# A decoder layer on one core: the first half's squares added by GpSimd, a third quad of weight sums made in DRAM, the gate's second-half residual added by DMA, and its root spread later

## The chip, the core and the metric

The kernel runs on one core of a Trainium2 chip. The metric is the time of one execution in device microseconds (us), the median of several runs. The engines are TensorE (PE in the profile; its weight loads are PEld), VectorE (DVE), ScalarE (ACT), GpSimd (POOL) and SyncE (SP). Each takes its instructions in order from a queue of its own. SP, ACT and POOL also issue DMAs; a DMA that adds to its destination (`accum_op`) is issued from POOL.

## The reference

One layer over 1024 positions of width 1024: a mixing block with its output projection, a squared-ReLU MLP and a gated embedding, each added to the residual.

```python
h = h + jnp.concatenate([y_a, y_b, y_c], axis=-1) @ w_out[i]
f = jnp.square(jax.nn.relu(rms_norm(h, norm2_g[i]) @ w_ff1[i]))
h = h + f @ w_ff2[i]
gate = jax.nn.sigmoid(rms_norm(h, norm3_g[i]) @ w_ple_gate[i])
h = h + gate * (p[i] @ w_ple_proj[i])
```

All is float32. `y_a`, `y_b` and `y_c` come from a gated convolution, eight heads of stick-breaking attention and a spatial-gating MLP.

## The kernel before, in words

Activations are held transposed, features on the 128 partitions and 512 positions (a half) in a tile. A float32 product is three matmuls of rounded parts: every operand is split into `hi` (a cast on ACT, line 138) and `lo` (a subtraction on DVE, line 139). The three large products after the mixing block are done as 2x2 blocks with seven block products instead of eight; their operands are sums of weight blocks ("S1" to "S4") beside plain blocks ("A11", "A12", "A22").

The order of instructions on each engine is set by a scheduler that runs a model of the program; `tc.issue_after(x)` holds an instruction behind x in that order. Tiles come from pools: `raw` (4 buffers), `sum` (6), `tmp` (12) and `w` (22) in the late part, where eight pairs of `w` hold the parts of `y` for a while.

The stages that the change touches:

- **Output projection** (lines 881 to 928). Two halves of eight blocks, in the order n = 0, 4, 1, 5, 2, 6, 3, 7. Each block is 24 matmuls into `o_ps`. SP loads its two weight tiles and the residual `xt`; DVE adds `o_ps` to `xt` (line 908); ACT stores it to `h_dram`, scales it to `hg` and squares it (line 845); POOL adds the square to `S2[h]` by an accumulating DMA (line 849). The last two squares of the second half are kept apart.
- **Roots.** `root_of` sums `S2` over the partitions on PE (`ms_ps`, line 858), DVE forms `ms` (861), POOL the power -1/2 `r` (174), DVE `diag` (866). `spread_root` spreads it by a matmul (`R_ps`, 873) and an ACT copy (874). The first half's root stands in PE's order behind the second half's third block.
- **Sums of weights** (`up_sums`, line 786). After the square of each block but the first of each half and the last two, one step of `STEPS` makes part of the sums of a quad in `u_sums`, in DRAM: copies on ACT's queue, accumulates on POOL's. Four steps make a quad; there are twelve chances for a step. Quads 0 and 1 are made so; for all later quads SP loads a block and POOL adds others to it in SBUF (`add_up`, line 798). `events` gives each load, add and split a place among the products of the up projection, seven slots to a quad, and `supply` issues them.
- **Up projection** (line 943 on). For each of 16 quads PE makes seven products; ACT copies the first bank to `v` (line 961) before PE adds to that bank again.
- **Gate** (line 1179 on). Seven products over four blocks j in the order of `GATE`. `gated` (1161) multiplies by the root, takes the sigmoid, multiplies by `pp` and adds the residual on DVE, then stores; the stores go from POOL except for two tiles. The second half's root is taken at product 1, j = 1, and spread at product 1, j = 3.

Of the kernel before, what the change touches and what calls it, by code (L numbers as in the profile page):

```python
# [10 lines left out]
ALU = mybir.AluOpType  # L11
# [5 lines left out]
KT = D // P  # L17
# [15 lines left out]
def hybrid_block(ctx: ExitStack, tc: tile.TileContext, a: dict):  # L33
# [5 lines left out]
    nc = tc.nc  # L39
# [130 lines left out]
    def cols(parts, sl):  # L170
        return parts[0][:, sl], parts[1][:, sl]
# [41 lines left out]
    S1 = halves("S1")  # L213
# [543 lines left out]
    def add(eng, out, x, y):  # L757
        return eng.tensor_tensor(out=out, in0=x, in1=y, op=ALU.add)  # L758
# [7 lines left out]
    def run(bank, w, b, first, last, part=slice(None)):  # L766


        w, b = w[part], b[part]
        for k, ((lh, ll), (rh, rl)) in enumerate(zip(w, b, strict=True)):  # L770
            for i, (l, r) in enumerate(((lh, rh), (lh, rl), (ll, rh))):
                done = nc.tensor.matmul(bank, l, r, start=first and k == 0 and i == 0,  # L772
                                        stop=k == len(b) - 1 and i == 2, skip_group_check=True)
        return done
# [5 lines left out]
    FIRST = (1, 2, 6, 5, 7, 3, 4)  # L780
    raw_of, up_pairs = {}, {}

    EARLY = 2
    u_sums = dram.tile([EARLY, 4, P, HT], F32, name="u_sums")

    def up_sums(i, behind_add, behind_act):
# [20 lines left out]
    for q in range(FT):  # L807
        base = 7 * (q - 1)
        sums = ((-6, load_up, "S1", "A21"), (-4, add_up, "S1", "A22"),
                (-4.1, load_up, "S2", "A11"), (-2, add_up, "S2", "S1"),  # L810
                (-1.1, load_up, "S3", "A11"), (1, add_up, "S3", "A21"),
                (0.1, load_up, "S4", "A12"), (2.1, add_up, "S4", "S2"))
        if q < EARLY:
            sums = tuple((at, load_up, to, to) for at, to in zip(
                ((2, 2.1, 3.4, 3.45), (-0.9, -0.89, 0.9, 2))[q], ("S2", "S1", "S3", "S4")))
        events += [(base + at, what, q, *args) for at, what, *args in sums + (
            (-2.1, load_up, "A11", "A11"),
            (3.8 if q == 0 else 2, load_up, "A12", "A12"), (4, load_up, "A22", "A22"))]
        for k, p in enumerate(UP if q else FIRST):
            events.append((base + k + 0.5 if q else (-3.5, -0.99, -0.98, -0.97, -0.96, -0.4, -0.3)[k],  # L820
                       pair_up, q, p))
# [18 lines left out]
    def late_squares(acc, src, first, by_dma=False, apart=False):  # L840
        if first:
            nc.scalar.activation(acc, src, AF.Square)
            return
        sq = late_slot("tmp", "sq")
        nc.scalar.activation(sq, src, AF.Square)
        if apart:
            return sq
        if by_dma:
            return nc.gpsimd.dma_start(acc, sq, accum_op=ALU.add)
        return add(nc.gpsimd, acc, acc, sq)  # L850
# [30 lines left out]
    for h in range(2):  # L881
        for n in (0, 4, 1, 5, 2, 6, 3, 7):
            end = h == 1 and n in (3, 7)
            if h == 1:

                if n == 5:
                    with tc.issue_after(block_end.ins):
                        diag = root_of([S2[0]], "20")
                elif n == 6:
                    with tc.issue_after(block_end.ins):  # L890
                        spread_root(diag, R2[0])
                supply({4: -12, 1: -10, 5: -8, 2: -6, 6: -4, 7: -3}.get(n, -100))
            wu = first_wu[n] if h == 0 and n in first_wu else plain_units(a["w_out"][n])
            if end:
                xt = fetch(a["xT"][n * P:(n + 1) * P, half[h]], "sum")
            else:
                xt = slot("xt")
                nc.sync.dma_start(xt, a["xT"][n * P:(n + 1) * P, half[h]])
            o_ps = late_bank("o_ps")
            block_end = product(o_ps, [(wu[k], y_parts[h][k]) for k in range(KT)])  # L900
            if h == 0:
                i = len(y_parts[1])
                src = fetch(y_dram[i, 1], "sum") if i < 6 else y_a[i - 6][1]
                y_parts[1].append(two_parts(src, lambda s: late_slot("w", f"y_{s}", F32R)))
            if h == 1 and n == 7:
                supply(-0.975)

            evicted = add(nc.vector, xt, o_ps, xt)
            nc.scalar.dma_start(h_dram[n, h], xt)
            t = hg[n][h] = late_slot("tmp", "hg")  # L910
            scaled = nc.scalar.activation(t, xt, AF.Copy, scale=g2[:, n:n + 1])
            summed = late_squares(S2[h], xt, n == 0, True, end)
            if end:
                last_sqs.append(summed)
            elif summed:
                up_sums(up_step[0], summed, scaled)
                up_step[0] += 1
            if h == 1 and n == 7:
                supply(-0.955)
            j = n % 4  # L920
            if h == 0:
                hn[1 if n < 4 else 2][j] = hn_pair(t)
            elif n >= 4:
                b11, b12, b21 = hg[j][0], hg[j][1], hg[n][0]
                t2 = late_slot("tmp", "t2")
                token_sums(b11, b12, b21, t, nc.vector, b11, t2, b12, b21)
                for p, src in ((6, t2), (5, b11), (7, b12), (3, t), (4, b21)):
                    hn[p][j] = hn_pair(src)
# [229 lines left out]
                parts = w_pair(src)  # L1158
                yield [unit(parts, k) for k in range(4)]

    def gated(n, h, src, t, c, sign=1.0):

        nc.vector.tensor_tensor(out=t, in0=src, in1=R3[h][:, c], op=ALU.mult)  # L1163
        nc.scalar.activation(t, t, AF.Sigmoid, scale=sign)
        nc.vector.tensor_tensor(out=t, in0=t, in1=pps[n, h][:, c], op=ALU.mult)  # L1165
        add(nc.vector, t, t, h_res[n][h][:, c])
        queue = nc.sync if (n, h) in ((KT - 1, 0), (KT - 2, 0)) else nc.gpsimd
        queue.dma_start(a["out"][n * P:(n + 1) * P, half[h]][:, c], t)

    def bring_pp(n, h):  # L1170
# [8 lines left out]
    for p in GATE:  # L1179
        for j in range(4):  # L1180

            cs = pieces if p in (7, 4) and j == 3 else whole
            banks = (d_bank.pop((MATE[p], j)) if p in MATE
                     else [late_bank("g_ps")[:, :c.stop - c.start] for c in cs])
            if p in (1, 3, 7):
                d_bank[p, j] = banks
            w_of.append(next(w_made, None))
            w = w_of.pop(0)
            if p == 2:
                bring_pp(j, 0)  # L1190
            elif p == 5:
                bring_pp(j, 1)
            elif p in (7, 4):
                bring_pp(j + 4, 1 if p == 7 else 0)
            for bank, c in zip(banks, cs):
                run(bank, w, [cols(b, c) for b in h3[p]], p not in MATE, p not in (1, 7))
                if p == 1:
                    v_of[j] = late_slot("tmp", "v")
                    nc.scalar.copy(v_of[j], bank)
                elif p == 2:  # L1200
                    gated(j, 0, bank, late_slot("tmp", "gt"), c)
                elif p == 6:
                    subtract(nc.vector, v_of[j], v_of[j], bank)
                elif p == 5:
                    e_of[j] = late_slot("tmp", "e")
                    add(nc.vector, e_of[j], bank, v_of[j])
                    t = late_slot("tmp", "gt")
                    add(nc.vector, t, d_bank.pop((3, j))[0], e_of[j])
                    gated(j, 1, t, t, c)
                elif p == 7:  # L1210
                    t = e_of[j][:, c]
                    add(nc.vector, t, bank, t)
                    gated(j + 4, 1, t, t, c, -1.0)
                elif p == 4:
                    t = v_of[j][:, c]
                    add(nc.vector, t, bank, t)
                    gated(j + 4, 0, t, t, c, -1.0)
            if p == 1:
                if j == 1:
                    diag = root_of([S3[1], last_sq[1]], "31")  # L1220
                elif j == 3:
                    spread_root(diag, R3[1])
                h3_pair(2, j + 4, 0)
                sum_h("12", "22", j)
            elif p == 2:
                h3_pair(3, j + 4, 1)
                sum_h("22", "11", j)
            elif p == 3:
                h3_sum(6, "22", j)
                sum_h("21", "22", j)  # L1230
            elif p == 6:
                h3_sum(5, "11", j)
            elif p == 5:
                h3_sum(7, "12", j)
            elif p == 7:
                h3_sum(4, "21", j)
# [62 lines left out]
```

## Time and profile before

| | before |
|---|---|
| runs, us | 1248.59, 1244.39, 1247.66; median 1247.66 |
| profiled execution, us | 1249.21 |
| its span, us | 1247.5 |
| mean granted PE clock | 0.981 |
| busy, share of the span | PE 96%, PEld 82%, DVE 71%, ACT 50%, POOL 31% |
| moved by DMA | 253.77 MB, mean 203 GB/s |

The profile is one execution. A row of its groups names line, engine, operation, output <- input, and the count; the waits name who waited for whom. In a timeline row stand start and duration in us, the instruction, and in brackets how long the engine was idle before it and what released it. `S<-sq` is the accumulate of a square, `raw<-in_w_ff` a load of MLP weights, `u_sums<-u_sums` an accumulate in DRAM.

### The profile page before, as it was taken

The numbers are of one execution on the slowest core, as the hardware profiler recorded it, in microseconds if no ns is written. First come the engines' busy times: TensorE is split into PE (matmuls) and PEld (weight loads), VectorE is DVE, ScalarE is ACT, GpSimd is POOL, SyncE is SP. The second block draws the span as 40 slices with busy tenths as digits, with TensorE's granted clock in tenths as the row PEclk, the third lists the DMA queues.
The fourth block names the chain that finished last, engine by engine and source line by source line (L and its number), as shares of the span: only waits on it lengthen the run. The fifth ranks groups of instructions, "written<-read, shape, count | busy, mean of one in ns | idle before, by whom it ended". The sixth has DMA issues, their size and how long they took to land. (4 is left out here: it accounts for less than half of the span.)

```text
span 1247.5 us, 17726 instructions
## 1 busy us (share of the span) xinstructions
PE 1202.3 (96%) x5852; PEld 1026.6 (82%) x5852; DVE 891.7 (71%) x1319; ACT 626.6 (50%) x1244; POOL 388.6 (31%) x408
## 2 busy tenths in 40 slices
PE   9999999999999996998999999999999999999896
PEld 7899898998888784787888888888888888888785
DVE  7746888879788643687887777777665567754687
ACT  7736677667555453553333333355544444446632
POOL 3324345355322111115445445331023301013301
PEclk9999899899999998899999999999999999999998
DMA  9603269898622489779999998868979985645743
GB/s 321 205 18 111 101 183 255 230 189 154 127 55 43 169 226 281 204 218 249 259 262 243 254 266 242 224 228 281 342 229 317 276 266 169 226 145 122 167 145 133
DMA packets 127484, 253.77 MB, mean 203 GB/s; under 512 B 14465, under 2 KB 21889, under 8 KB 126753
## 3 DMA queue, kind: packets, MB, share of 16 engines
q1 hardware_dynamic: 96288, 170.70, 41.7%
q0 software_dynamic: 28032, 58.88, 24.6%
q10 hardware_dynamic: 3072, 23.07, 5.0%
q8 instruction: 46, 0.75, 0.3%
q14 instruction: 46, 0.37, 0.1%
HBM read 191.25 MB, written 91.23 MB: 226 GB/s over the span
## 5 line engine op out<-in xcount | busy, mean ns | idle before, releaser
L139 DVE TENSOR_TENSOR w_lo<-raw,w_hi 128x512 fp32r<-128x512 f32 x280 | 251.3, 901 | 93.6 <-ACT w_hi L138 93.2
L138 ACT CAST w_hi<-raw 128x512 fp32r<-128x512 f32 x280 | 171.5, 619 | 236.9 <-PE d_ps L772 116.8
L772 PE MATMUL f_ps<-hn_hi,w_hi 128*128 128x512 f32 x448 | 175.3, 392 | 3.9 <-ACT v L961 3.9
L772 PE MATMUL f_ps<-hn_lo,w_hi 128*128 128x512 f32 x448 | 174.8, 390 | 0.0
L772 PE MATMUL d_ps<-f_hi,w_hi 128*128 128x512 f32 x448 | 174.8, 390 | 0.0
L772 PE MATMUL f_ps<-hn_hi,w_lo 128*128 128x512 f32 x448 | 174.7, 391 | 0.0
L772 PE MATMUL d_ps<-f_hi,w_lo 128*128 128x512 f32 x448 | 174.3, 389 | 0.0
L772 PE MATMUL d_ps<-f_lo,w_hi 128*128 128x512 f32 x448 | 174.3, 389 | 0.0
L426 DVE TENSOR_TENSOR_SCAN rem<-rem 128x128 f32<-128x128 f32 (+3 forms) x64 | 91.5, 1435 | 17.5 <-ACT rem L421 16.6
L772 PEld LDWEIGHTS f_ps<-hn_hi,w_hi 128*128 128x128 f32 x448 | 84.5, 189 | 21.9 <-ACT v L961 4.3
L772 PEld LDWEIGHTS f_ps<-hn_lo,w_hi 128*128 128x128 f32 x448 | 84.5, 189 | 17.9 <-issue 0.2
L772 PEld LDWEIGHTS f_ps<-hn_hi,w_lo 128*128 128x128 f32 x448 | 84.4, 188 | 17.8
L772 PEld LDWEIGHTS d_ps<-f_hi,w_hi 128*128 128x128 f32 x448 | 84.1, 188 | 17.7 <-issue 0.2
L772 PEld LDWEIGHTS d_ps<-f_lo,w_hi 128*128 128x128 f32 x448 | 84.1, 188 | 17.7 <-issue 0.2
L772 PEld LDWEIGHTS d_ps<-f_hi,w_lo 128*128 128x128 f32 x448 | 84.1, 188 | 17.4
L165 PE MATMUL qkv_ps<-whi,xn_hi 128*128 128x384 f32 x256 | 92.7, 362 | 1.9 <-DVE V L142 1.8
L166 PE MATMUL qkv_ps<-wlo,xn_hi 128*128 128x384 f32 x256 | 89.6, 350 | 0.0
L167 PE MATMUL qkv_ps<-whi,xn_lo 128*128 128x384 f32 x256 | 89.3, 349 | 0.0
L139 DVE TENSOR_TENSOR f_lo<-raw,f_hi 128x512 fp32r<-128x512 f32 x112 | 77.2, 718 | 11.1 <-ACT f_hi L138 10.6
L138 ACT CAST f_hi<-raw 128x512 fp32r<-128x512 f32 x112 | 66.9, 620 | 29.0 <-DMA raw<-f_dram 25.9
L429 POOL TENSOR_TENSOR wt<-wt,rem 128x127 f32<-128x127 f32 (+4 forms) x40 | 45.9, 1159 | 81.6 <-DVE rem L426 42.1
L174 POOL TENSOR_TENSOR rs<-ss,mhalf 128x4 f32<-128x4 f32 x32 | 42.1, 1314 | 78.4 <-DVE ss L346 78.4
(250 smaller groups left out, 2692.3 us busy)
## 6 DMA issues: line engine op xcount, KB each, us to landing
raw<-in_w_ff SPq DMA_DIRECT2D x152, 256.0 KB, 4.1
raw<-f_dram SPq DMA_DIRECT2D x112, 256.0 KB, 5.1
raw<-w_sums SPq DMA_DIRECT2D x64, 256.0 KB, 4.2
f_dram<-f SPq DMA_DIRECT2D x48, 256.0 KB, 4.0
f_dram<-t SPq DMA_DIRECT2D x48, 256.0 KB, 3.8
w_sums<-in_w_ff POOLq DMA_DIRECT2D x8, 1024.0 KB, 11.5
w_sums<-w_sums POOLq DMA_DIRECT2D x8, 1024.0 KB, 12.5
raw<-in_w_out SPq DMA_DIRECT2D x28, 256.0 KB, 5.5
```

The costliest lines, as they stand in the source:

```text
L138: last_hi[0] = nc.scalar.copy(hi, src)
L139: low.tensor_tensor(out=lo, in0=src, in1=hi, op=ALU.subtract)
L165: nc.tensor.matmul(ps, lh, rh, start=first and i == 0, stop=False)
L166: nc.tensor.matmul(ps, lh, rl, start=False, stop=False)
L167: done = nc.tensor.matmul(ps, ll, rh, start=False, stop=last and i == len(terms) - 1)
L174: last_power[0] = nc.gpsimd.tensor_tensor(out=out, in0=in_, in1=mhalf[:, :n], op=ALU.pow)
L426: nc.vector.tensor_tensor_scan(out=back, data0=back, data1=back, initial=1.0, op0=ALU.mult, op1=ALU.bypass)
L429: done = (nc.vector if on_vector else nc.gpsimd).tensor_tensor(out=wt[:, :W - 1], in0=wt[:, :W - 1], in1=rem[:, 1:W], op=ALU.mult)
L772: done = nc.tensor.matmul(bank, l, r, start=first and k == 0 and i == 0, stop=k == len(b) - 1 and i == 2, skip_group_check=True)
```

## The change

Four edits.

1. The seven squares of the first half are added to `S2[0]` by a POOL instruction; those of the second half are added by DMA as before.
2. `EARLY` is 3: the four steps that are left make the sums of quad 2 in DRAM too, in the second half of the output projection. Their loads get places of their own, and quad 2 has no `add_up` any more.
3. In `gated`, for the second half, an accumulating DMA from POOL adds the residual, and SP stores the result.
4. `spread_root` for the gate's second half moves from product 1, j = 3 to behind the last matmul of product 2, j = 1.

```diff
--- before.py
+++ after.py
@@ -780,7 +780,7 @@
     FIRST = (1, 2, 6, 5, 7, 3, 4)
     raw_of, up_pairs = {}, {}
 
-    EARLY = 2
+    EARLY = 3
     u_sums = dram.tile([EARLY, 4, P, HT], F32, name="u_sums")
 
     def up_sums(i, behind_add, behind_act):
@@ -812,7 +812,7 @@
                 (0.1, load_up, "S4", "A12"), (2.1, add_up, "S4", "S2"))
         if q < EARLY:
             sums = tuple((at, load_up, to, to) for at, to in zip(
-                ((2, 2.1, 3.4, 3.45), (-0.9, -0.89, 0.9, 2))[q], ("S2", "S1", "S3", "S4")))
+                ((2, 2.1, 3.4, 3.45), (-0.9, -0.89, 0.9, 2), (-1.1, -0.5, 0.9, 2))[q], ("S2", "S1", "S3", "S4")))
         events += [(base + at, what, q, *args) for at, what, *args in sums + (
             (-2.1, load_up, "A11", "A11"),
             (3.8 if q == 0 else 2, load_up, "A12", "A12"), (4, load_up, "A22", "A22"))]
@@ -909,7 +909,7 @@
             nc.scalar.dma_start(h_dram[n, h], xt)
             t = hg[n][h] = late_slot("tmp", "hg")
             scaled = nc.scalar.activation(t, xt, AF.Copy, scale=g2[:, n:n + 1])
-            summed = late_squares(S2[h], xt, n == 0, True, end)
+            summed = late_squares(S2[h], xt, n == 0, h == 1, end)
             if end:
                 last_sqs.append(summed)
             elif summed:
@@ -1158,13 +1158,16 @@
                 parts = w_pair(src)
                 yield [unit(parts, k) for k in range(4)]
 
-    def gated(n, h, src, t, c, sign=1.0):
+    def gated(n, h, src, t, c, sign=1.0, by_dma=False):
 
         nc.vector.tensor_tensor(out=t, in0=src, in1=R3[h][:, c], op=ALU.mult)
         nc.scalar.activation(t, t, AF.Sigmoid, scale=sign)
         nc.vector.tensor_tensor(out=t, in0=t, in1=pps[n, h][:, c], op=ALU.mult)
-        add(nc.vector, t, t, h_res[n][h][:, c])
-        queue = nc.sync if (n, h) in ((KT - 1, 0), (KT - 2, 0)) else nc.gpsimd
+        if by_dma:
+            nc.gpsimd.dma_start(t, h_res[n][h][:, c], accum_op=ALU.add)
+        else:
+            add(nc.vector, t, t, h_res[n][h][:, c])
+        queue = nc.sync if by_dma or (n, h) in ((KT - 1, 0), (KT - 2, 0)) else nc.gpsimd
         queue.dma_start(a["out"][n * P:(n + 1) * P, half[h]][:, c], t)
 
     def bring_pp(n, h):
@@ -1193,7 +1196,7 @@
             elif p in (7, 4):
                 bring_pp(j + 4, 1 if p == 7 else 0)
             for bank, c in zip(banks, cs):
-                run(bank, w, [cols(b, c) for b in h3[p]], p not in MATE, p not in (1, 7))
+                done = run(bank, w, [cols(b, c) for b in h3[p]], p not in MATE, p not in (1, 7))
                 if p == 1:
                     v_of[j] = late_slot("tmp", "v")
                     nc.scalar.copy(v_of[j], bank)
@@ -1206,11 +1209,11 @@
                     add(nc.vector, e_of[j], bank, v_of[j])
                     t = late_slot("tmp", "gt")
                     add(nc.vector, t, d_bank.pop((3, j))[0], e_of[j])
-                    gated(j, 1, t, t, c)
+                    gated(j, 1, t, t, c, by_dma=True)
                 elif p == 7:
                     t = e_of[j][:, c]
                     add(nc.vector, t, bank, t)
-                    gated(j + 4, 1, t, t, c, -1.0)
+                    gated(j + 4, 1, t, t, c, -1.0, True)
                 elif p == 4:
                     t = v_of[j][:, c]
                     add(nc.vector, t, bank, t)
@@ -1218,11 +1221,12 @@
             if p == 1:
                 if j == 1:
                     diag = root_of([S3[1], last_sq[1]], "31")
-                elif j == 3:
-                    spread_root(diag, R3[1])
                 h3_pair(2, j + 4, 0)
                 sum_h("12", "22", j)
             elif p == 2:
+                if j == 1:
+                    with tc.issue_after(done.ins):
+                        spread_root(diag, R3[1])
                 h3_pair(3, j + 4, 1)
                 sum_h("22", "11", j)
             elif p == 3:
```

The scheduler gives another order in places. On DVE, at the end of the output projection's first half, `xt_1225` and `xt_1239` are the evictions of that half's last two blocks and `xt_1253` that of the second half's first; `w_lo_1261` is the split of the second weight tile of the second half's second block, `w_lo_1279` and `w_lo_1282` those of its third, `w_lo_1294` the first of its fourth. Before:

```order
L139 TENSOR_TENSOR w_lo_1261_5529<-raw_1259_5526,w_hi_1260_5528 128x512
L758 TENSOR_TENSOR xt_1225_5376<-o_ps_1226_5378,xt_1225_5376 128x512
L139 TENSOR_TENSOR w_lo_1279_5596<-raw_1277_5593,w_hi_1278_5595 128x512
L139 TENSOR_TENSOR hn_lo_1232_5417<-hg_1229_5409,hn_hi_1231_5416 128x512
L139 TENSOR_TENSOR w_lo_1282_5602<-raw_1280_5599,w_hi_1281_5601 128x512
L758 TENSOR_TENSOR xt_1239_5432<-o_ps_1240_5434,xt_1239_5432 128x512
L139 TENSOR_TENSOR w_lo_1294_5655<-raw_1292_5652,w_hi_1293_5654 128x512
L139 TENSOR_TENSOR hn_lo_1246_5473<-hg_1243_5465,hn_hi_1245_5472 128x512
L139 TENSOR_TENSOR w_lo_1297_5661<-raw_1295_5658,w_hi_1296_5660 128x512
L758 TENSOR_TENSOR xt_1253_5488<-o_ps_1254_5490,xt_1253_5488 128x512
```

And now:

```order
L758 TENSOR_TENSOR xt_1225_5376<-o_ps_1226_5378,xt_1225_5376 128x512
L139 TENSOR_TENSOR w_lo_1261_5529<-raw_1259_5526,w_hi_1260_5528 128x512
L139 TENSOR_TENSOR hn_lo_1232_5417<-hg_1229_5409,hn_hi_1231_5416 128x512
L139 TENSOR_TENSOR w_lo_1279_5596<-raw_1277_5593,w_hi_1278_5595 128x512
L758 TENSOR_TENSOR xt_1239_5432<-o_ps_1240_5434,xt_1239_5432 128x512
L139 TENSOR_TENSOR w_lo_1282_5602<-raw_1280_5599,w_hi_1281_5601 128x512
L139 TENSOR_TENSOR hn_lo_1246_5473<-hg_1243_5465,hn_hi_1245_5472 128x512
L139 TENSOR_TENSOR w_lo_1294_5657<-raw_1292_5654,w_hi_1293_5656 128x512
L758 TENSOR_TENSOR xt_1253_5488<-o_ps_1254_5490,xt_1253_5488 128x512
```

Each eviction has moved ahead of one split of weights. SP's loads of `xt` have moved ahead of one weight load in the same way.

On ACT, around the second quad's copy `v` in the up projection: `S2_1139` is the second half's root, `f` and `v_1406` belong to the first quad. The casts from `w_hi_1449` on, before, are those of quad 2; `raw_1421`, `raw_1414`, `raw_1430` and `raw_1442` are its four sums. Before:

```order
L138 CAST w_hi_1443_6206<-raw_1427_6132 128x512
L874 COPY S2_1139_5040<-R_ps_1434_6172 128x512
L936 ACTIVATE v_1406_6027<-v_1406_6027 128x512
L138 CAST w_hi_1449_6230<-raw_1421_6119 128x512
L936 ACTIVATE f_1407_6029<-f_1407_6029 128x512
L138 CAST w_hi_1452_6251<-raw_1414_6105 128x512
L936 ACTIVATE f_1431_6153<-f_1431_6153 128x512
L138 CAST w_hi_1455_6272<-raw_1430_6151 128x512
L138 CAST w_hi_1458_6294<-raw_1451_6248 128x512
L138 CAST w_hi_1461_6316<-raw_1442_6204 128x512
L961 COPY v_1445_6211<-f_ps_1438_6188 128x512
```

Now, where quad 2's sums are `raw_1428`, `raw_1432`, `raw_1443` and `raw_1450`:

```order
L138 CAST w_hi_1441_6208<-raw_1425_6135 128x512
L138 CAST w_hi_1448_6233<-raw_1428_6153 128x512
L138 CAST w_hi_1452_6255<-raw_1432_6173 128x512
L138 CAST w_hi_1455_6276<-raw_1443_6212 128x512
L874 COPY S2_1139_5040<-R_ps_1433_6176 128x512
L936 ACTIVATE v_1406_6035<-v_1406_6035 128x512
L936 ACTIVATE f_1407_6037<-f_1407_6037 128x512
L936 ACTIVATE f_1429_6155<-f_1429_6155 128x512
L138 CAST w_hi_1458_6298<-raw_1451_6253 128x512
L138 CAST w_hi_1461_6320<-raw_1450_6251 128x512
L961 COPY v_1444_6215<-f_ps_1437_6192 128x512
```

Three of the four casts of sums have moved ahead of the root's copy, and one is left before `v`.

On PE, the spread of the gate's second-half root (`R_ps`) stands 16 matmuls later than before, and nothing else of PE's order in that stage is changed.

## The prediction

> **What bounds the kernel now.** I read the page first, then the list of who waited for whom on TensorE (PE), then the timeline around each long wait. The page's share for PE says what there is to win at all.
>
> ```profile
> span 1247.5 us, 17726 instructions
> PE 1202.3 (96%) x5852; PEld 1026.6 (82%) x5852; DVE 891.7 (71%) x1319; ACT 626.6 (50%) x1244; POOL 388.6 (31%) x408
> ```
>
> PE is idle 1247.5 - 1202.3 = 45.2 us of the span, so time can only come from its waits and from matmuls that run slowly behind a wait. The columns of the next view are: total us, times, longest.
>
> ```profile
> PE ms_ps L858 <- DMA S<-sq: 8.8, 1, 8.8
> PE f_ps L772 <- ACT v L961: 3.9, 1, 3.9
> PE R_ps L873 <- DVE diag L866: 3.5, 2, 3.3
> PE o_ps L167 <- DVE w_lo L139: 2.5, 2, 1.9
> ```
>
> Three single waits of 8.8, 3.9 and 3.3 us stand out, and three of the edits touch what each of them waits for. The first is the root of the first half's squares, in PE's timeline (start, duration, in brackets the idle time before):
>
> ```profile
> 484.27 0.50 PE L167 MATMUL o_ps<-y_hi,w_lo 128*128 128x512 f32 x1 [1.86 <-DVE w_lo L139]
> ...
> 489.36 0.40 PE L167 MATMUL o_ps<-y_hi,w_lo 128*128 128x512 f32 x1
> 498.55 1.87 PE L858 MATMUL ms_ps<-ones,S 128*128 128x2 f32 x8 [8.80 <-DMA S<-sq]
> 500.28 0.77 PE L165 MATMUL o_ps<-y_hi,w_hi 128*128 128x512 f32 x1
> ...
> 506.37 0.39 PE L167 MATMUL o_ps<-y_hi,w_lo 128*128 128x512 f32 x1
> ```
>
> PE was there at 489.36 + 0.40 = 489.75. Behind the wait 14 matmuls take 506.37 - 500.28 = 6.09 us, 0.43 each. In the gate stage 28 take 6.40 us, 0.229 each (rows below), so the slow stretch costs 6.09 - 14 x 0.229 = 2.9 us more. Behind the wait of 1.86 us there is none: the 21 steps from 484.27 to 489.36 take 0.24 each.
>
> **Part by part. A, the first half's squares on GpSimd.** What the first root waited for, on three engines, and below it GpSimd's own add of the same shape in a later stage (min/median/max, ns):
>
> ```profile
> 488.86 0.69 DVE L758 TENSOR_TENSOR xt<-o_ps,xt 128x512 f32<-128x512 f32 x1 [1.75 <-DMA xt<-in_xT]
> 490.58 0.61 ACT L845 ACTIVATE sq<-xt 128x512 f32<-128x512 f32 x1
> 491.49 0.89 POOL L849 DMA_DIRECT2D S<-sq  x1 [4.19 <-ACT sq L845]
> L758 POOL TENSOR_TENSOR S<-S,sq x12: 1282/1298/3354, 1032.6 to 1153.2; 128x512 f32<-128x512 f32 x12
> ```
>
> The last square's accumulate is issued at 491.49 and releases PE at 498.55. An add of 1.30 us at the same place ends at 492.8, 3.25 us after the eviction's end (488.86 + 0.69 = 489.55). With nothing else changed PE would wait 492.8 - 489.75 = 3.05 us instead of 8.80.
>
> Two things are changed besides. First, the seven accumulates leave a stage that is short of transfers: DVE sits in its queue waiting for `xt`, and SyncE's queue waits for the weight sums' accumulates before it can issue the next `xt`.
>
> ```profile
> DVE xt L758 <- DMA xt<-in_xT: 27.8, 9, 6.0
> ```
> ```profile
> SPq L701 <- DMA u_sums<-u_sums: 8.1, 2, 4.3
> ```
>
> From 425 to 535 GpSimd's DMA queue holds these (the first row: packets, MB, share of 16 engines):
>
> ```profile
> q0 software_dynamic: 2736, 4.98, 27.9%
> ...
> S<-sq POOLq DMA_DIRECT2D x12, 256.0 KB, 5.1
> ...
> u_sums<-in_w_ff POOLq DMA_DIRECT2D x4, 256.0 KB, 8.3
> u_sums<-u_sums POOLq DMA_DIRECT2D x4, 256.0 KB, 6.7
> ```
>
> That is 0.279 x 110 us over 20 accumulates, 1.53 us of all DMA engines each; seven fewer free 10.7 us before the root. Second, the scheduler moves each eviction of `xt` one weight split ahead on DVE, and its load one weight load ahead on SyncE (the order of DVE in the section on the change). The last eviction now stands before the split for the second half of PE's last block. PE thus reaches the root about 0.6 + 12 x 0.229 = 3.4 us after that eviction, and the sum is ready 3.25 us after it: the root's own wait goes to about nothing, whenever `xt` lands. What can be left is a wait for that split. PE wants it at 489.75 - 2.75 = 487.0; with `xt` landing as now it is there at 490.15, 3.1 us late. I take `xt` 2 us sooner, since it passes a weight load in the queue and the traffic is less; with the like of the 1.86 us wait elsewhere, 2.5 us stay in all, in pieces too short for slow matmuls. **A gains 8.80 + 1.86 - 2.5 + 2.9 = 11.1 us.** At most it is 10.66 + 2.9 = 13.6.
>
> The lower end comes from GpSimd and DVE running side by side:
>
> ```profile
> 1145.85 2.32 DVE L139 TENSOR_TENSOR w_lo<-raw,w_hi 128x512 fp32r<-128x512 f32 x1 [1.90 <-ACT w_hi L138]
> ```
> ```profile
> 1043.97 3.35 POOL L758 TENSOR_TENSOR S<-S,sq 128x512 f32<-128x512 f32 x1 [4.36 <-ACT sq L845]
> ```
>
> One of GpSimd's adds took 3.35 us while DVE was dense, and a split of 0.69 us took 2.32 beside another. With the last add at 3.35 (2.05 more) and `xt` no sooner, 3.1 + 2.05 + 1.86 = 7.0 us of idle stay and the slow matmuls too: a gain of 3.7 us. The Trainium skill (SBUF — State Buffer, "Who interferes with whom") says that the port pair of these two engines is an exclusive lock, the later one being blocked for the whole instruction; these two rows agree. By that rule as the only effect, with the 2.05 us added to the wait, A would be 9.1 us and the kernel 2 us slower than I forecast.
>
> **B, third quad's sums in DRAM.** Four copies on ScalarE's queue and four accumulates on GpSimd's join the second half of this stage. At 1.53 us an accumulate, and a copy between nothing and the same, that is 6.1 to 12.2 us of transfers. The stage's windows (length, busy times of PE, PEld, DVE, ACT and POOL, then granted clock, DMA share, GB/s):
>
> ```profile
> 425.00:485.00 60.00, 56.45 (x245) 45.84 (x246) 28.22 (x45) 28.65 (x50) 7.76 (x9) 1.00 0.92 270
> 485.00:505.00 20.00, 11.20 (x40) 8.82 (x39) 9.11 (x15) 7.82 (x14) 6.61 (x8) 0.69 0.99 254
> 505.00:545.00 40.00, 39.71 (x170) 32.04 (x170) 32.76 (x54) 28.22 (x52) 4.36 (x5) 0.98 0.75 211
> ```
>
> From 485 to 545 the transfers fill 0.99 x 20 + 0.75 x 40 = 49.8 us. Less two of the removed accumulates (3.1), and with the new ones, it is 52.8 to 58.9, in 60 - 11.1 = 48.9 us: 4 to 10 us too much, if all of it had to be done there. It need not: before 485 there is now room, and the sums are wanted only some 20 us after 545. So B costs 0 to 10 us; I take 3, nearer the low end, since only loads of `w_out` and `xt` hold PE here. What stands behind the new waits on GpSimd is the second root's `r`; its cover is in the row of the slower rival below.
>
> **C, the same sums at the second quad.** ScalarE's copy `v` stands behind the casts of the third quad's sums, made by accumulates in SBUF:
>
> ```profile
> 563.71 0.62 ACT L138 CAST w_hi<-raw 128x512 fp32r<-128x512 f32 x1 [7.79 <-DMA raw<-raw]
> ...
> 568.75 0.62 ACT L138 CAST w_hi<-raw 128x512 fp32r<-128x512 f32 x1 [1.82 <-DMA raw<-raw]
> ```
> ```profile
> 569.91 0.50 PE L772 MATMUL f_ps<-hn_hi,w_hi 128*128 128x512 f32 x1 [3.88 <-ACT v L961]
> ...
> 574.83 0.39 PE L772 MATMUL f_ps<-hn_hi,w_lo 128*128 128x512 f32 x1
> ```
>
> The 14 steps to 574.83 take 4.92 us, 1.7 more than at 0.229. Now these casts read plain loads, three of them before the root's copy, and the four accumulates are gone from GpSimd's queue. The wait of 3.88 us can go whole; what is late next is the cast of the fourth sum, for which I keep 0.5. **C gains 5.1 us**, between 0 and 5.6.
>
> **D, gate's root of the second half spread later.** From the chain of waits and from PE's timeline:
>
> ```profile
> 1162.55 5.51 DMA hg<-hg
> ...
> 1170.56 0.70 DVE diag L866
> ```
> ```profile
> 1167.65 0.39 PE L772 MATMUL g_ps<-h_lo,w_hi 128*128 128x512 f32 x1
> ...
> 1171.86 1.37 PE L772 MATMUL g_ps<-h_hi,w_lo 128*128 128x512 f32 x1
> ...
> 1175.47 0.39 PE L772 MATMUL g_ps<-h_hi,w_hi 128*128 128x512 f32 x1
> ...
> 1181.87 0.39 PE L772 MATMUL g_ps<-h_lo,w_hi 128*128 128x512 f32 x1
> ```
>
> The 7 steps from 1171.86 to 1175.47 take 3.61 us, 2.0 above full speed; the spread's own second pass is in the first of them, so I count 1.7. In PE's order the spread moves 16 matmuls back: PE reaches it at 1167.88 + 16 x 0.229 = 1171.5, and `diag` ends at 1171.26. The margin is 0.3 us, and the chain to `diag` holds accumulates of 5.5 us that can shift; I keep 0.7 us. **D gains 3.3 + 1.7 - 0.7 = 4.3**, between 3 and 5.
>
> **E, gate's residual by DMA.** It takes 9 adds off DVE, where PE had no wait in the gate stage, and puts 9 accumulates on GpSimd's queue and 9 stores on SyncE's. PE's last matmul, DVE's last multiply of the second half, and the times to landing of the squares' accumulates:
>
> ```profile
> 1237.62 0.28 PE L772 MATMUL g_ps<-h_hi,w_lo 128*128 128x256 f32 x1
> ```
> ```profile
> 1231.17 0.42 DVE L1165 TENSOR_TENSOR e<-e,raw 128x256 f32<-128x256 f32 x1
> ```
> ```profile
> DMA to landing us min/median/max: 3.4/5.1/7.4
> ```
>
> Even at 7.4 us the last accumulate is in at 1231.6 + 0.9 + 7.4 = 1239.9 (0.9 for the issue, as above), and a second such transfer ends at 1247.3, inside the span; at 5.1 each it ends at 1242.7. Behind the last matmul one multiply of 0.4 us moves ahead: gain 0.2, between -2 and 0.4.
>
> **The sum** is 11.1 - 3 + 5.1 + 4.3 + 0.2 = 17.7 us. The profiled execution took 1249.21 us, its span and 1.7 us around it, which gives 1231.5; it is 1.55 us above the median of the runs, 1247.66, and on that the forecast is 1230.0 us.
>
> **The rivals.** *The added transfers bound the second half* (0.18): B costs its 10 us, 1237.0. For it speaks the DMA share of 0.99 up to 505; against it, that the sums can wait. *Loads of `xt` stay late and the add is slowed* (0.13): A is 3.7, 1237.4. For it speaks the 27.8 us of waits for `xt`; against it, seven accumulates fewer. *Both together* (0.05): 3.7 - 10 + 5.1 + 4.3 + 0.2 = 3.3 us, 1244.4, within 0.3%, which is about what a measurement of this kernel can tell from no change.
>
> *Slower: DVE's waits for `xt` come through to PE* (0.04). Each eviction now stands in front of a split that PE needs half a block, 2.75 us, sooner. Of DVE's 9 waits only 1.86 us reached PE so far. If each cost that half block, A would be 11.1 - 24.7, the sum -7.0, and the time 1254.7. It decides where `xt` lands less than 2.75 us sooner against PE than now; SyncE's issuing it one load earlier speaks against. A late second root is no such case:
>
> ```profile
> POOL r L174 <- DVE ms L861: 21.3, 2, 16.0
> ```
>
> GpSimd idled 16 us ahead of that `r`, so the accumulates now queued before it cost PE nothing until they are 16 us late.
>
> **Chances and range.** My forecast has 0.60. The range runs from 1225, near the sum of the best ends (13.6 + 5.6 + 5 + 0.4 = 24.6), to 1239, beyond the two rivals of 1237. Faster by over 0.3%: 0.60 + 0.18 + 0.13 = 0.91; within: 0.05; slower: 0.04.
>
> **What would show it.** In the new trace the PE wait for `ms_ps` at the first root is under 1 us, with no run of 0.43-us matmuls behind it; waits for `w_lo` in 465 to 490 sum to about 2.5 us. The wait for `v` at the second quad is gone, and the casts of the third quad wait for plain loads. The second gate spread waits under 1 us. It would be wrong if PE's waits for `w_lo` in the second half of this stage sum to over 5 us, if `ms_ps` still waits 3 us or more, or if the stores of the second half end last.

## The result, and the profile after

The changed kernel took 1236.59 us (median of four runs, 1236.15 to 1237.46) where the kernel before took 1246.39 beside it: a ratio of 0.9922, 95% interval 0.9901 to 0.9942. The forecast was 1230.0 with a range to 1239. The direction was right and the gain, 9.8 us, a little over half of the 17.7 forecast. Three times more, beside the experiments, the kernel before had medians of 1245.95, 1244.49 and 1245.13; its profiled execution, 1249.21, lies 3 to 5 us above all of these. That matters below.

The page of the profiled execution after (1236.95 us):

```profile
span 1234.4 us, 17751 instructions
PE 1201.2 (97%) x5852; PEld 1027.2 (83%) x5852; DVE 885.5 (72%) x1310; ACT 627.4 (51%) x1244; POOL 393.3 (32%) x408
```

PE is idle 33.2 us instead of 45.2. Of the three long waits none is left; in the list of PE's waits three others have grown instead:

```profile
PE o_ps L167 <- DVE w_lo L139: 3.6, 1, 3.6
...
PE o_ps L165 <- ACT w_hi L138: 2.8, 1, 2.8
...
PE R_ps L873 <- DVE diag L866: 1.6, 1, 1.6
```

**The first root** waits for nothing, and its neighbours run at full speed (PE's timeline, then POOL's last add):

```profile
493.86 0.39 PE L167 MATMUL o_ps<-y_hi,w_lo 128*128 128x512 f32 x1
494.09 0.95 PE L858 MATMUL ms_ps<-ones,S 128*128 128x2 f32 x8
494.90 0.49 PE L165 MATMUL o_ps<-y_hi,w_hi 128*128 128x512 f32 x1
```
```profile
490.98 1.30 POOL L758 TENSOR_TENSOR S<-S,sq 128x512 f32<-128x512 f32 x1 [4.05 <-ACT sq L845]
```

**The new waits.** All three follow a late `xt`, the last two after shorter waits of DVE's for it (0.8 and 2.6 us in all). The longest, over three engines (SP, DVE, PE, each from its timeline):

```profile
467.29 0.80 SPq L701 DMA_DIRECT2D raw<-u_sums  x2
468.18 0.38 SPq L898 DMA_DIRECT2D xt<-in_xT  x1
```
```profile
474.01 0.69 DVE L758 TENSOR_TENSOR xt<-o_ps,xt 128x512 f32<-128x512 f32 x1 [8.27 <-DMA xt<-in_xT]
474.62 0.68 DVE L139 TENSOR_TENSOR w_lo<-raw,w_hi 128x512 fp32r<-128x512 f32 x1
```
```profile
475.35 0.80 PE L167 MATMUL o_ps<-y_hi,w_lo 128*128 128x512 f32 x1 [3.58 <-DVE w_lo L139]
475.94 0.63 PE L165 MATMUL o_ps<-y_hi,w_hi 128*128 128x512 f32 x1
...
481.06 0.47 PE L166 MATMUL o_ps<-y_lo,w_hi 128*128 128x512 f32 x1
```

SP issues `xt` only behind two reloads of sums that had waited for their accumulate; DVE stands 8.27 us before the eviction, and the split that PE wants is next in its queue. Behind the wait 12 matmuls take 5.12 us, 0.43 each. The lists of waits from 425 to 535 show both (DVE, then SP's queue):

```profile
DVE xt L758 <- DMA xt<-in_xT: 19.6, 10, 8.3
```
```profile
SPq L701 <- DVE w_lo L139: 64.3, 29, 8.3
SPq L701 <- DMA u_sums<-u_sums: 10.1, 2, 6.6
```

DVE waits for `xt` 8 us less than before, but the longest single wait is longer, and the accumulates hold SP 2 us more. The stage's windows, cut as in the prediction:

```profile
425.00:485.00 60.00, 53.91 (x224) 44.06 (x225) 31.98 (x45) 29.41 (x52) 9.71 (x10) 0.94 0.83 253
485.00:505.00 20.00, 20.00 (x93) 16.66 (x92) 14.71 (x22) 10.81 (x20) 7.84 (x8) 1.00 0.95 260
505.00:545.00 40.00, 35.60 (x156) 28.40 (x154) 32.36 (x53) 28.13 (x51) 6.95 (x8) 0.96 0.95 257
```

PE loses 6.1 us up to 485, where it lost 3.6 before, none around the root, where it lost 8.8, and 4.4 after it, where it lost 0.3. Of the 2.5 us more up to 485, 1.4 are only a shift: the stage opens with a wait of 2.5 to 2.7 us in both (PE's, for `cv_acc`), and because the stage starts 1.2 us later now, nearly all of it falls behind 425.

**The second quad and the gate.** `v` is copied with no wait in front of it, the second spread of the gate finds `diag` 2.7 us old, and PE's last matmul starts at 1225.99, 8.4 us before the end (ACT, DVE, PE):

```profile
559.86 0.58 ACT L961 COPY v<-f_ps 128x512 f32<-128x512 f32 x1
```
```profile
1161.61 0.69 DVE L866 TENSOR_TENSOR diag<-ident,r 128x512 f32<-128x512 f32 x1 [5.50 <-POOL r L174]
```
```profile
1165.03 1.02 PE L873 MATMUL R_ps<-diag,ones 128*128 128x512 f32 x2
...
1225.99 0.28 PE L772 MATMUL g_ps<-h_hi,w_lo 128*128 128x256 f32 x1
```

### The profile page after: what moved, and what is told of

It reads as the page before. It is cut to its first block, busy times and chain, and to the rows that moved or that the text cites. A ratio compares the mean times of both kernels' runs of the same rounds, so it can differ in the third digit from the quotient of the medians.

```text
span 1234.4 us, 17751 instructions
## 1 busy us (share of the span) xinstructions
PE 1201.2 (97%) x5852; PEld 1027.2 (83%) x5852; DVE 885.5 (72%) x1310; ACT 627.4 (51%) x1244; POOL 393.3 (32%) x408
## 3 DMA queue, kind: packets, MB, share of 16 engines
q0 software_dynamic: 27664, 57.05, 24.7%
## 4 chain that ended last, share of the span: by engine, by line
PE 84%; DVE 6%; DMA 4%; issue 2%; ACT 2%; POOL 1%; SPq 0%; ACTq 0%; DVEq 0%; POOLq 0%
PE f_ps L772 25%; PE d_ps L772 25%; PE g_ps L772 6%; PE qkv_ps L165 3%; PE qkv_ps L166 3%; PE qkv_ps L167 3%; DMA xt<-in_xT 2%; PE av L469 2%; DVE rem L426 2%; PE w_tr L451 2%; PE cv_ps L165 1%; PE cv_ps L166 1%; PE cv_ps L167 1%; PE vu_ps L167 1%; PE vu_ps L165 1%
## 5 line engine op out<-in xcount | busy, mean ns | idle before, releaser
L139 DVE TENSOR_TENSOR w_lo<-raw,w_hi 128x512 fp32r<-128x512 f32 x280 | 239.8, 860 | 83.5 <-ACT w_hi L138 80.8
L772 PEld LDWEIGHTS f_ps<-hn_hi,w_lo 128*128 128x128 f32 x448 | 84.8, 189 | 17.9
L772 PEld LDWEIGHTS f_ps<-hn_hi,w_hi 128*128 128x128 f32 x448 | 84.8, 189 | 17.7 <-issue 0.2
L772 PEld LDWEIGHTS f_ps<-hn_lo,w_hi 128*128 128x128 f32 x448 | 84.7, 189 | 17.9 <-issue 0.2
L772 PEld LDWEIGHTS d_ps<-f_hi,w_hi 128*128 128x128 f32 x448 | 84.1, 188 | 17.7 <-issue 0.2
L772 PEld LDWEIGHTS d_ps<-f_lo,w_hi 128*128 128x128 f32 x448 | 84.1, 188 | 17.7 <-issue 0.2
L758 POOL TENSOR_TENSOR S<-S,sq 128x512 f32<-128x512 f32 x19 | 27.4, 1440 | 170.1 <-ACT sq L845 170.1
```

What stands on the lines that cost most here:

```text
L139: low.tensor_tensor(out=lo, in0=src, in1=hi, op=ALU.subtract)
```

## The experiments

Fourteen profiles are compared by four marks in PE's timeline: the last matmul of the convolution's product (`cv_ps`, the stage ahead of the output projection), the first of the down projection (`d_ps`), the first and the last of the gate (`g_ps`), and the end of the span. The first column is the first mark's time; up to there all fourteen run the same instructions. Times in us; the ratio is to the kernel before on the same chip, from all runs.

| kernel, edits in it | first mark | to `d_ps` | gate | tail | median | ratio (95%) |
|---|---|---|---|---|---|---|
| before, none | 423.2 | 422.8 | 84.3 | 9.9 | 1246.39 | 1 |
| o_squares, 1 | 420.5 | 420.0 | 84.3 | 9.0 | 1240.65 | 0.9934 (0.9906-0.9961) |
| o_gate, 3 | 422.5 | 423.0 | 80.3 | 9.3 | 1244.55 | 0.9999 (0.9985-1.0012) |
| o_spread, 4 | 423.2 | 422.1 | 79.1 | 9.9 | 1242.70 | 0.9976 (0.9962-0.9990) |
| u_squares, 2 3 4 | 423.7 | 423.1 | 79.1 | 9.3 | 1241.78 | 0.9976 (0.9954-0.9998) |
| u_quad, 1 3 4 | 425.0 | 416.2 | 79.1 | 8.4 | 1237.15 | 0.9920 (0.9896-0.9943) |
| u_gate, 1 2 4 | 422.8 | 414.2 | 79.1 | 9.0 | 1234.46 | 0.9913 (0.9884-0.9943) |
| u_spread, 1 2 3 | 418.4 | 413.3 | 80.1 | 8.4 | 1235.03 | 0.9917 (0.9889-0.9945) |
| after, all | 424.4 | 415.1 | 79.1 | 8.4 | 1236.59 | 0.9922 (0.9901-0.9942) |
| again, all | 422.0 | 412.2 | 79.1 | 8.4 | 1235.56 | 0.9912 (0.9894-0.9930) |
| x_hold, all and reloads later | 421.7 | 417.8 | 79.2 | 8.7 | 1236.03 | 0.9918 (0.9898-0.9938) |
| x_raw5, all and a fifth buffer | 422.4 | 417.9 | 79.2 | 8.4 | 1235.08 | 0.9909 (0.9877-0.9941) |
| x_act, all and `xt` on ACT's queue | 423.5 | 414.4 | 79.1 | 8.7 | 1233.63 | 0.9912 (0.9876-0.9947) |
| x_both, all and both of these | 418.6 | 416.4 | 79.1 | 8.5 | 1231.78 | 0.9899 (0.9870-0.9927) |

Up to `d_ps` the gate's edits 3 and 4 play no part, so rows that agree in 1 and 2 are the same code there: 422.1 to 423.0 with neither, 423.1 with edit 2, 416.2 and 420.0 with edit 1, 412.2 to 415.1 with both. One profile is thus good to 1 to 4 us; "again" was run to see this.

> The changed kernel itself once more, beside the next three on one chip, for the scatter between its executions: a second profile of each stage, and the median of more runs. If the scatter that the others showed (7 us between the ten profiles before the output projection, where all run the same code) is the kernel's own, its runs spread over some 8 us too, about 1229 to 1239.

It took 1235.56 (1231.33 to 1236.76), a spread of 5.4 us where 8 were expected: most of the scatter is the kernel's own. Its profile has PE waits of 4.0 for `w_lo`, 2.2 for `diag`, 1.2 for `w_hi`, the same places as the first.

### One edit at a time: squares and quad

The first theory (queue): what A fell short by sits in SP's queue, where `xt` stands behind reloads that wait for accumulates. Its rival is the prediction's own (transfer): the third quad's transfers bound the second half.

```diff
-            summed = late_squares(S2[h], xt, n == 0, h == 1, end)   # u_squares: edit 1 undone
+            summed = late_squares(S2[h], xt, n == 0, True, end)
-    EARLY = 3                                                       # u_quad: edit 2 undone
+    EARLY = 2
-            summed = late_squares(S2[h], xt, n == 0, True, end)     # o_squares: on the kernel before
+            summed = late_squares(S2[h], xt, n == 0, h == 1, end)
```

> The changed kernel (1236.6 us) with only edit 1 undone: the first half's squares are added by DMA again. Queue theory: of the changed kernel's gain in the output projection (about 3.5 us on PE's clock between the last matmul of the stage before and the second root) nearly all is edit 1's, because a late xt holds up PE either way; undone it costs 3 to 5 us, 1240 to 1242. Transfer theory: edit 1 is worth its 11 us and the third quad's added transfers take 7.5 of them back; undone, the stage loses 11 us, about 1247.5, slower than the kernel before's 1246.4.

> The changed kernel with only edit 2 undone: the third quad's sums are made by accumulates in SBUF again (EARLY = 2). Queue theory: the four copies and four accumulates cost the output projection 0 to 1 us, and the wait for v at the second quad comes back with some 4.4 us, 1240 to 1241. Transfer theory: the stage gets 7 us shorter and the wait for v costs 4.4: about 1234.

> The kernel before (1246.4 us) with edit 1 alone. Queue theory: the root's wait of 8.8 us goes, but xt stays late behind the reloads of the weight sums in SyncE's queue, and now stands before PE's weight splits on DVE: 3 to 5 us gained, 1241.5 to 1243.5, with a new PE wait for w_lo of 3 us or more that follows a DVE wait for xt. Transfer theory: without the third quad's transfers it gains its 11 us, about 1235.5, with no such wait. Add theory (GpSimd's adds slow DVE's splits): w_lo splits of over 2 us beside each add, PE waits spread over the seven blocks, 2 to 4 us gained.

u_squares took 1241.78: 0.9976 of the kernel before where all four edits have 0.9922 and 0.9912, so edit 1 is worth 0.59%, 7 us; alone, in o_squares, 0.66% or 8 us (5 to 12). Both lie between the theories' numbers. u_squares excludes the transfer theory's 1247.5. The time of u_quad, 1237.15, would still allow its 1234, but u_quad's way from the first mark to the second root's spread (`R_ps`), which holds all the added transfers, is 127.3 us without them and 125.4 to 128.6 with them (the four profiles with all of edits 1 and 2 and nothing else in this stage), not 7 us shorter. And in o_squares, without any third quad, the wait for the sum of squares has gone and the new ones are there:

```profile
PE o_ps L167 <- DVE w_lo L139: 5.9, 2, 5.4
PE R_ps L873 <- DVE diag L866: 5.8, 2, 3.3
...
PE o_ps L165 <- ACT w_hi L138: 2.6, 1, 2.6
```

The add theory falls too: GpSimd's adds take 1.28 to 1.30 us in all seven places. DVE does pay for them: beside each of the seven one split takes 1.26 to 1.45 us instead of 0.68, six times an `hn_lo`, once a `w_lo`. But PE waits behind none of these (POOL, then DVE, in the changed kernel):

```profile
484.90 1.29 POOL L758 TENSOR_TENSOR S<-S,sq 128x512 f32<-128x512 f32 x1 [7.13 <-ACT sq L845]
```
```profile
485.30 1.44 DVE L139 TENSOR_TENSOR hn_lo<-hg,hn_hi 128x512 fp32r<-128x512 f32 x1 [1.61 <-ACT hn_hi L138]
486.67 0.68 DVE L139 TENSOR_TENSOR w_lo<-raw,w_hi 128x512 fp32r<-128x512 f32 x1
```

The split beside the add ends 0.55 us after it and takes twice its 0.68. The Trainium skill (SBUF — State Buffer, "Who interferes with whom") calls the port pair that the two share an exclusive lock; the trace agrees, 0.76 us here. The prediction's row of 2.32 us shows less than was read from it: that split started at 1145.85, 0.15 us ahead of the add beside it (1146.00), so it was not the later of the two.

### The late xt: three tries at its cause

First the reloads. SP gets two of the four behind the load of `xt` for the fifth block of the second half, and two behind that for the sixth:

```diff
-                nc.sync.dma_start(xt, a["xT"][n * P:(n + 1) * P, half[h]])
+                xt_load = nc.sync.dma_start(xt, a["xT"][n * P:(n + 1) * P, half[h]])
...
-        raw_of[q, to] = fetch(src, tag)
+        if q == 0 and of[0] == "S":
+            with tc.issue_after(xt_load.ins):
+                raw_of[q, to] = fetch(src, tag)
+        else:
+            raw_of[q, to] = fetch(src, tag)
```

> The changed kernel with one thing more: SyncE issues the reloads of the first quad's four sums only behind the load of xt for the fifth block of the second half, some eight blocks later than now, so that no xt stands behind a load that waits for an accumulate in DRAM. The same transfers are made, later. Queue theory: the DVE wait of 8.3 us for xt goes, the PE wait of 3.6 us for w_lo and the 2.4 us of slow matmuls behind it go too: 5 to 6 us faster, about 1231. Transfer theory: the second half is the crowded one and gets four loads more: 1237 to 1240.

1236.03: no gain, the queue theory's 1231 is missed. The 8.3 us wait is gone (the longest of DVE's for `xt` is 4.0), but PE waits 4.9 us for `w_lo` in four pieces and 5.8 for `w_hi` later. The 5.8 may come in part from the edit itself: that cast waits for a load of `w_out` that SP issues at 513.77, behind the moved reloads, and that takes 8.44 us to land. The chain of waits shows why `xt` stays late (start, duration):

```profile
469.23 0.69 DVE w_lo L139
...
469.94 0.33 SPq L701
...
470.32 7.17 DMA xt<-in_xT
...
478.12 0.69 DVE w_lo L139
```

This is a ring: a split frees a `raw` buffer, SP loads the next weights into it and issues `xt` behind that, DVE evicts when `xt` has landed, and its next split stands behind the eviction. From split to split it goes 10.0, 8.9 and 5.8 us (459.22, 469.23, 478.12, 483.90), where a block of 24 matmuls takes PE 5.5. Most of each round is the landing of `xt`: 8.25, 7.17 and 4.05 us of it. That the reloads only lengthened one round is the reading that fits; this run does not prove it. Two kernels loosen the ring, one at the buffers, one at SP's queue, and a third does both:

```diff
-LATE = {"w": 22, "raw": 4, "sum": 6, "tmp": 12, "R": 2}                       # x_raw5, x_both
+LATE = {"w": 22, "raw": 5, "sum": 5, "tmp": 12, "R": 2}
-                nc.sync.dma_start(xt, a["xT"][n * P:(n + 1) * P, half[h]])    # x_act, x_both
+                nc.scalar.dma_start(xt, a["xT"][n * P:(n + 1) * P, half[h]])
```

> The changed kernel (1236.6 us) with five buffers for loaded weights instead of four, and five instead of six for weight sums (the space is the same). Ring theory, formed after x_hold: SyncE loads the next weights into a buffer that DVE's split frees, the load of xt stands behind that load, DVE's eviction waits for xt, and the next split stands behind the eviction. Round that ring go 6 to 9 us where a block of PE takes 5.5. With a buffer more SyncE is a load ahead, DVE's evictions stand a split later, PE's waits for w_lo and w_hi in the stage (6.4 us, and 4 us of slow matmuls) go mostly: 1229 to 1232. Transfer theory: the DMA engines are full whatever the order, no change, 1236 to 1238.

> The changed kernel with xt loaded by ScalarE's queue instead of SyncE's. Ring theory: xt no longer stands behind loads that wait for DVE's splits, and lands sooner: PE waits of 6.4 us for w_lo and w_hi go down, 1230 to 1234, unless ScalarE's own order (the load stands behind the block before's square) makes another ring of the same length, which would leave 1236. Transfer theory: no change, 1236 to 1238.

> The changed kernel with five buffers for loaded weights and five for sums, and xt loaded by ScalarE's queue: both cures together. Ring theory: no PE wait for w_lo, w_hi or diag over 1 us between the first block and the second root, so no slow matmuls there: stage to the first matmul of the down projection 408 to 411 us behind the stage before, 3 to 6 us shorter than the changed kernel's 414.2 (mean of three), 1228 to 1232. Against it: each cure alone left some 2 to 4 us of other short waits and slow matmuls, so that the two may again give 414, 1234.

The waits do what the ring theory says, the times do not: x_raw5 (1235.08) and x_both (1231.78, with 416.4 to `d_ps` where 408 to 411 was expected) miss, and only x_act (1233.63) is where it was expected. In x_raw5 those for `w_lo`, `w_hi` and `diag` shrink from 8.0 us to 1.1, and others take their place:

```profile
PE ms_ps L858 <- POOL S L758: 2.0, 1, 2.0
...
PE f_ps L772 <- ACT hn_hi L138: 1.0, 1, 1.0
...
PE o_ps L167 <- DVE w_lo L139: 0.8, 2, 0.6
PE f_ps L772 <- DVE hn_lo L139: 0.7, 2, 0.5
...
PE R_ps L873 <- DVE diag L866: 0.3, 1, 0.3
```

With the evictions a split later, the last square's add comes after PE, and the root waits 2.0 us; the 13 matmuls behind that run at 0.43 us. A second slow stretch stands around the second root, where 24 matmuls of two columns take 5.1 us instead of 2.7. Ten microseconds there, in x_raw5 and in the changed kernel (PE's busy time comes first after the length, the granted clock is third from the end):

```profile
540.00:550.00 10.00, 10.00 (x36) 8.95 (x37) 7.91 (x14) 3.66 (x8) 1.41 (x1) 0.51 0.48 142
```
```profile
542.00:552.00 10.00, 10.00 (x51) 8.58 (x50) 8.84 (x15) 2.29 (x4) 2.34 (x2) 0.83 0.62 189
```

So in x_raw5 the waits that were saved came back as slow matmuls, and the stage was no shorter. x_act keeps 4.4 for `diag`, behind two evictions whose `xt` ScalarE issues late. No ratio of the three differs from the changed kernel's by more than the intervals; x_both's median is the lowest, 3.8 us below "again" on the same chip, and its runs spread from 1228.11 to 1239.36. Whether it is faster stays open.

### The gate: edits 3 and 4

```diff
-                if j == 1:                                # u_spread: edit 4 undone
-                    with tc.issue_after(done.ins):
-                        spread_root(diag, R3[1])
...
-                    gated(j, 1, t, t, c, by_dma=True)     # u_gate: edit 3 undone
+                    gated(j, 1, t, t, c)
-                    gated(j + 4, 1, t, t, c, -1.0, True)
+                    gated(j + 4, 1, t, t, c, -1.0)
```

In u_spread the call stands again under product 1, j = 3; o_spread and o_gate are the kernel before with one of the edits alone.

> The changed kernel with only edit 4 undone: the gate's root of the second half is spread 16 matmuls earlier again. By both theories the PE wait of 3.3 us and some 1.9 us of slow matmuls are back: 5.2 us slower, 1241 to 1242. If the accumulates of edit 3 on GpSimd's queue had moved the root instead, under 2 us slower.

> The changed kernel with only edit 3 undone: DVE adds the gate's residual of the second half and GpSimd's queue stores it. By both theories PE's matmuls end at the same time, and the tail behind the last matmul is 8.4 us with edit 3 and 9.9 us without: 0 to 1.5 us slower, 1236.6 to 1238.

> The kernel before (1246 us) with edit 4 alone. Order theory: PE reaches the gate's second spread 16 matmuls later and diag is there; the gate takes 79.1 us to its last matmul instead of 84.3, some 5 us faster, 1240 to 1242. If GpSimd's accumulates of the gate's operands are what ended later in the kernel before, and edit 3 or the others moved them, part of the wait stays: 81 us or more.

> The kernel before (1246 us) with edit 3 alone. Order theory: nothing ahead of the gate's second spread has moved, so diag ends 18 us after the gate's first matmul as in the kernel before, and the gate takes 84.3 us: 1245 to 1246, with the tail shorter by up to 1.5. If this edit is what made diag come 3 us sooner in the changed kernel without edit 4, the gate takes 80 us here: 1241 to 1242.

With edit 4 the gate takes 79.1 us in every profile. Without it, 84.3 (before, o_squares) or 80.1 and 80.3 (u_spread, o_gate). The wait at the spread, in u_spread and in o_gate:

```profile
1154.50 1.12 PE L873 MATMUL R_ps<-diag,ones 128*128 128x512 f32 x2 [0.68 <-DVE diag L866]
```
```profile
1168.55 1.12 PE L873 MATMUL R_ps<-diag,ones 128*128 128x512 f32 x2 [0.94 <-DVE diag L866]
```

`diag` ends 17.9 and 18.0 us behind the gate's first matmul in the profiles of before and o_squares, and 15.2 to 15.8 in the twelve others, though in o_gate no instruction ahead of it stands elsewhere than in the kernel before. The medians side with the short wait: o_spread gains 3 us (1 to 5), not 5.2; undoing edit 4 costs nothing that shows; and o_gate, whose profile has a gate 4 us shorter than before's, has the time of the kernel before (0.9999). That the two chains of accumulates were late draws is the likely reading, since a real 4 us would stand in o_gate's median. It also fits that both late profiles are long executions of their kernels (1249.21 where the medians are 1244.5 to 1247.7, and 1242.98, the longest of o_squares' seven), while o_gate's, 1244.43, is at its median. Against it stands that the two are just the two kernels with neither edit 3 nor 4. Each kernel but one was profiled once; it is argued, not shown. Edit 3 shortens the tail by 0.6 us (9.9 to 9.3, 9.0 to 8.4), too little for the medians.

## Why the prediction was right, and where it was wrong

**What bounds, and the direction: right.** PE's waits are where the time came from; PE's busy time fell by 1.1 us only, and its idle time by 12.

**A, mis-sized: 11.1 forecast, 7 to 8 measured.** The root's wait goes to nothing, as forecast, and the waits for `w_lo` alone keep to the 5 us that I had named as the limit. The term that failed is the residue: "2.5 us stay in all, in pieces too short for slow matmuls". The two profiles of the changed kernel and those of u_gate and u_spread, the same code here, have 7.4 to 8.2 us of waits for `w_lo`, `w_hi` and `diag` in this stage. I took `xt` to land 2 us sooner because it is asked for earlier and less was moved. From issue to landing its 14 loads gained 0.4 us in the median, and 0.1 in o_squares, where the seven accumulates fewer are the only change in traffic (the kernel before, then the changed one):

```profile
DMA to landing us min/median/max: 3.0/5.2/8.4
```
```profile
DMA to landing us min/median/max: 3.0/4.8/5.9
```

The rest of a round, the ring of split, buffer, load and eviction, sets when `xt` is asked for. Nor are the pieces too short: three of the four profiles have 11 to 17 matmuls at 0.43 us behind these waits, up to the second root. One step of this is argued, not shown: x_raw5 and x_both take most of these waits away and gain no time up to `d_ps`, so the waits are where A fell short in the profiles, but no run gives the missing us back. Of the 7 to 8 measured, 0.9 are not in this stage at all: the tail is shorter by that with edit 1 (9.9 to 9.0, 9.3 to 8.4), which I had not counted and whose cause is open.

**The rival on the slower side had the right mechanism.** DVE's waits do come through to PE, at three to seven places, not nine; at the first large one it costs 2.7 to 5.4 us. That took some 5 us of A, not 24.7. The rival of the late `xt` and the slowed add, whose gain of 10.3 us came nearest to the 9.8, was right on `xt` and wrong on the add. The rival of the added transfers, with a gain of 10.7 about as near, falls with u_quad: a near number with the wrong reason.

**B, forecast at a loss of 3, and C, a gain of 5.1: together near nothing in the medians.** Undoing both costs 0.3 us (0.9920 against 0.9917), give or take 3. In the profiles the way to `d_ps` is 418.1 without edit 2 (two) and 413.7 with it (four), so up to 4 us are possible. Parted at the second root's spread, the profiles say more. Behind it, where C lies, it is 286.5 to 286.8 us to `d_ps` in all nine profiles with edit 2, 288.8 and 288.9 in the two with edit 1 only, and 289.1 to 293.0 in the three with neither: beside edit 1, C is worth some 2.3 us, not 5.1. Ahead of it B shows no loss beside edit 1 (the 127.3 and 131.2 without edit 2, the 125.4 to 128.6 with it); without edit 1 the stage is longer with the third quad (136.6 in u_squares, one profile, against 130.0 to 133.1). C rested on one wait of 3.9 us for `v`. In the five profiles without edit 2 it is 3.9 (before), 3.9 (o_gate), 0.8 (o_spread) and absent in o_squares and u_quad, where a wait of 1.3 us for DVE's `f` stands at its place; from the lists of PE's waits of before and o_spread:

```profile
PE f_ps L772 <- ACT v L961: 3.9, 1, 3.9
```
```profile
PE f_ps L772 <- ACT v L961: 0.8, 1, 0.8
```

**D, 4.3 forecast: 3 (1 to 5) alone, nothing that shows on top of the others.** The step was right in kind: no profile with edit 4 waits there; its size came from a wait of 3.3 us that two other profiles without the edit have as 0.7 and 0.9. **E, 0.2: small, as forecast,** but 0.6 in the profiles, where I had put the most at 0.4.

**The step under all of these** was to count every wait of one profile at full length and to carry the sum to the median unchanged. That profile was 3 to 5 us above the kernel's medians, and two of the three long waits in it are short or absent in other profiles that run the same code up to there. The row that could have warned stood in the prediction: landings of 3.4 to 7.4 us for the same accumulate. What is left of the gain: 7 to 8 from edit 1, 0 to 3 from edit 4, and from 2 and 3 too little for the medians, some 2 and 0.6 by the profiles.

## What to carry to other kernels

When a wait at a join is taken away, ask what sets the arrival of the engine's next operand: here a ring of in-order queues and few buffers, whose longest link, a landing of some 5 us, seven transfers fewer hardly shortened. A wait whose end is a DMA's landing counts with its mean, so take a second profile, or a median, before giving it its full length in a sum. And where an edit moves an eviction in front of a split, price the eviction's operand at the split's deadline.

## What was not expected of the hardware

The first mark, up to which all kernels run the same instructions, lies between 418.4 and 425.0 us, a scatter two thirds the size of the gain. The granted clock up to there goes with it, 1.00 at 418.4, 0.99 at 418.6 and 420.5 and 0.98 from 421.7 on; the windows of u_spread, which has 418.4, and of u_quad, which has 425.0 (the clock is third from the end):

```profile
0.00:419.20 419.20, 403.41 (x2348) 366.13 (x2348) 325.26 (x530) 258.64 (x608) 164.58 (x173) 1.00 0.56 150
```
```profile
0.00:425.80 425.80, 410.64 (x2348) 373.13 (x2348) 325.91 (x530) 258.37 (x608) 163.20 (x173) 0.98 0.55 148
```

A wait's length does not say whether slow matmuls follow. The stage's opening wait, for `cv_acc`, is 2.5 to 3.1 us in all fourteen profiles, with the same matmuls of 512 columns behind it; 7 or 8 of them at 0.43 us follow in six, none in eight. In u_spread 10.9 us of waits in eight pieces, the longest 2.7, are followed by none up to the second root; in x_raw5 a single wait of 2.0 us, with a root of small matmuls behind it, is followed by 13. And no wait is needed: in the window of the changed kernel from 542 to 552 (shown with x_raw5's) PE is busy for 10.00 of 10.00 us and the clock is 0.83; eight slow matmuls stand there behind the second root's 24 small ones. The Trainium skill (TensorE: Matmul & The Clock Gate, "HAM oscillation — how this bites in real kernels") has the rule that idle gaps beyond about 3.4 us are what re-throttles. The runs do not agree, by the gaps of 2.0 to 3.1 us just named; its Part 1 has the activity windows run free of the kernel's start, which would fit the scatter, but no run here shows it.
